# GpSimd in written order, more weights prepared in the output projection, copies behind the mean, and other first loads in a two-layer float32 trunk

## The chip, the cores and the metric

The kernel runs on one core of a Trainium2 chip. The metric is the device time of one execution in microseconds (us). The core's engines are named as in the profile: PE (TensorE; PEld is its weight load), DVE (VectorE), ACT (ScalarE), POOL (GpSimd) and SP (SyncE, which here only issues the loads of weights). A difference of about 0.3% is what a measurement of this kernel can tell from no change.

## What is computed

272 tokens (16 learned ones ahead of 256) of width 1024 go through two layers. Each layer is a gated feed-forward, a mixer, and a second feed-forward, each with a norm before and after it and a residual; the mixer of the first layer is a short convolution, that of the second a differential attention of eight heads. The output is the last 256 tokens.

```python
for i in range(DEPTH):                      # DEPTH = 2
    f = swiglu(rms_norm(h, ln_ffn1[i, 0]), ffn1_w_gu[i], ffn1_w_down[i])
    h = h + 0.5 * rms_norm(f, ln_ffn1[i, 1])
    hn = rms_norm(h, ln_mix[i, 0])
    m = short_conv_mixer(hn, ...) if i == 0 else diff_attention_mixer(hn, ...)
    h = h + rms_norm(m, ln_mix[i, 1])
    f = swiglu(rms_norm(h, ln_ffn2[i, 0]), ffn2_w_gu[i], ffn2_w_down[i])
    h = h + 0.5 * rms_norm(f, ln_ffn2[i, 1])
return h[:, N_META:]
# in diff_attention_mixer, per head: a = softmax(s0) - lam * softmax(s1); o = rms_norm(a @ v) * (1 - lambda_init)
```

## The kernel before

Activations stand transposed: the feature on the 128 partitions, the tokens in the columns. Every product is done in three matmuls per weight tile of 128 by 128: both factors are split into an upper part (`hi`, rounded) and a lower part (`lo`, the rest), and hi*hi, hi*lo and lo*hi are summed in PSUM (`mm3`, L232).

The weights of the twelve products are twelve streams of tiles in the order of their use: `guf0`, `dnf0` (first feed-forward), `cin`, `cout` (convolution), `guf1`, `dnf1`, `guf2`, `dnf2`, `qkv`, `o` (attention), `guf3`, `dnf3`. A chunk of 16 tiles (1 MB) is one load by SP into one of three `raw` buffers; half a chunk, a group of 8 tiles, is prepared by `prepare` (L145): ACT casts `raw` to `hi` (L168), DVE subtracts to get `lo` (L172). There are seven `hi` and seven `lo` buffers. `stream` (L210) runs through the tiles of a stream and calls `prepare` at given places; in the streams `qkv` and `o` that is at the second tile of a group, and at the sixth only if fewer than four groups are ready.

A product that follows a norm begins before the norm's factor is known: for each k (128 features) the first six output tiles are multiplied, six hi*hi, six with the weights' lo, six with the activations' lo (L257, L259, L261). At tile `LATE` (50) the mean comes (`ms`), then its square root on ACT and the reciprocal on DVE, and the outputs are scaled by it (`done`).

At the very start SP loads the eight activation tiles `h` and between them the first 48 weight tiles, six tiles for each k. `guf0`'s first six groups are cast in two halves of four tiles each. 18 small matmuls (`warm_start`) run on PE meanwhile.

The steps of the attention's heads (`Head`) are hung between the tiles of `qkv` and `o` by a table (`HEAD_AT`, `STEPS`): `scores` (`pss`), `most` and `exps` (the softmax), `mix` (the two softmaxes to `w`, on DVE, with a memset of a gap in `w` on POOL), `turn` (PE transposes `w` to `pw`), `turned` (ACT copies it to `wT`), `values` (`po`), `squares` (ACT), `mean` (POOL), `root` (two steps on ACT), `newton` (four small steps on POOL), `scale` (ACT, `o`), `give` (PE transposes `o` to `pt`), `upper`, `lower` (split into the activations of stream `o`). After head 7's `root`, ACT loads the table of the square root, since the next functions need it. At tile 214 DVE takes the reciprocal `rho` of the norm before, and at tiles 216 to 218 and 230 to 234 POOL makes the eight residual tiles `h_f` (`Post.h`, L413) that are needed after the attention.

What sets the order: PE's instructions stand in written order throughout; DVE's and ACT's too in the stretches between `hold` and `let_go`, the attention among them; a scheduler orders POOL's instructions everywhere, and the loads go in the order of `prepare`, as `raw` buffers come free.

Behind the product `o`, `Post` takes the squares of the eight output tiles (ACT), sums them (DVE here, `acc`), sums over partitions by two matmuls with ones (`ms_out`), takes the root (`sz`), and copies the tiles, scaled by a gain, to `f` (L378). The residual, `z`, is formed on DVE from these, and its first tile (`z_f_hi`) starts `guf3`.

Of the kernel before, what the change touches and what calls it, by code (L numbers as in the profile page):

```python
# [14 lines left out]
AF = mybir.ActivationFunctionType  # L15
# [3 lines left out]
P = 128  # L19
# [18 lines left out]
MORE_AT = (2, 6, 7)  # L38
FIRST_AT = (0, 1, 3, 4, 5, 7)
TAIL = 4  # L40
LATER = ("cin", "guf1", "guf2", "qkv", "guf3")
WARM_N = 256
START_WARM = 18
# [49 lines left out]
def trunk_kernel(ctx, tc, a, out):  # L93
# [11 lines left out]
    ctx.enter_context(tc.manual_schedule(engines={mybir.EngineType.PE}))  # L105
    held = []

    def hold():
        if not held:
            held.append(tc.manual_schedule(engines={mybir.EngineType.DVE, mybir.EngineType.Activation}))  # L110
            held[0].__enter__()

    def let_go():
        if held:
            held.pop().__exit__(None, None, None)

    ctx.callback(let_go)
# [33 lines left out]
    def prepare(defer=None):  # L151
        if not queue:
            return
        label, c, g = queue.pop(0)
        if (label, c) not in raws:
            load(label, c)
        raw = raws[label, c]
        hi = wsp.tile([P, HC * P], F32R, tag="hi", name=f"hi_{label}_{c}_{g}")
        lo = wsp.tile([P, HC * P], F32R, tag="lo", name=f"lo_{label}_{c}_{g}")
        both = raw[:, g * HC * P : (g + 1) * HC * P]  # L160

        gain = GAINS[label][:, 0:1] if label in LATER and c == g == 0 else None
        parts = ((0, KO), (KO, HC)) if gain is not None else ((0, HC // 2), (HC // 2, HC)) if label == "guf0" and c < 3 else ((0, HC),)
        for s, e in parts:
            sl = slice(s * P, e * P)
            if gain is None or s:
                with queued(last["sqrt"]):
                    nc.scalar.copy(hi[:, sl], both[:, sl])  # L168

                def lower(sl=sl):  # L170
                    with queued(last["rs"]):
                        nc.vector.tensor_tensor(lo[:, sl], both[:, sl], hi.bitcast(F32)[:, sl], ALU.subtract)  # L172

                lower() if defer is None else defer(lower)
            else:
                nc.scalar.activation(hi[:, sl], both[:, sl], AF.Copy, scale=gain)
                nc.vector.scalar_tensor_tensor(lo[:, sl], both[:, sl], gain, hi.bitcast(F32)[:, sl], ALU.mult, ALU.subtract)
        groups[label, c, g] = hi, lo
# [21 lines left out]
    def at_2(f):  # L200
        at(2, f)

    def run_later(i=None):
        for j in sorted(later) if i is None else (i,):
            for f in later.pop(j, ()):
                f()

    def stream(label, pre=None):
        order = a["streams"][label][1]
        for i, km in enumerate(order):  # L210
# [7 lines left out]
            if label in (*LATER, "guf0") and i <= LATE:  # L218
                pass
            elif label == "qkv" or label == "o":  # L220

                if j == 1 and ahead(label, i) < HIS - 1 or j == 5 and ahead(label, i) < AHEAD and i > LATE + 3 * KD:
                    prepare(at_2)
            elif j == HC // 2 and ahead(label, i) < HIS - 1:
                prepare()
            elif j == 2 and (i > len(order) - 2 * HC and after.get(label) in LATER or ahead(label, i) < AHEAD):
                prepare()
# [62 lines left out]
    for k in range(KD):  # L290
        nc.sync.dma_start(h[k], a["xT"][:, k, :])
        if k == 0:
            nc.scalar.dma_start(gains, a["gains"])
        i, end = k * KO, (k + 1) * KO
        while i < end:
            c, j = divmod(i, CH)
            e = min(CH, j + end - i)
            load("guf0", c, slice(j * P, e * P))
            i += e - j
    small = const.tile([P, 4 * HD + 1], F32, name="small")  # L300
    rope = const.tile([P, 2, T], F32, name="rope")

# [113 lines left out]
    class Pre:  # L416
# [8 lines left out]
        def before(self, i):  # L425
            k, j = divmod(i, KO)
            if i < KD * KO and j == 0:
                if k == 0:
                    run_later()
                    hold()  # L430
                if self.post is None:
                    if k == 0:
# [146 lines left out]
    def attention(name, before, hs):  # L579
# [75 lines left out]
        class Head:  # L655
# [98 lines left out]
            def root(self):  # L754
                _, vv, y, _ = self.st
                nc.scalar.activation(y, vv, AF.Ln)
                nc.scalar.activation(y, y, AF.Exp, scale=-0.5)
                if self.hd == NH - 1:
                    table(AF.Sqrt, y)

            def newton(self):
                _, vv, y, t2 = self.st
# [14 lines left out]
            def upper(self):  # L777
# [2 lines left out]
                lo = actp.tile([P, SEQ], F32R, tag=f"al{hd}", name=f"a_{name}_{hd}_lo")  # L780
                nc.scalar.activation(hi, self.pt[:, :SEQ], AF.Copy, scale=gsub)
                acts[hd] = hi, lo

            def lower(self):
                hi, lo = acts[self.hd]
# [21 lines left out]

        def parts(i):
            if i == LATE:
                for hd, head in enumerate(heads):  # L810
                    for step, late in (STEPS if hd < NH - 1 else LAST_STEPS).items():
                        if hd == NH - 2 and late >= STEPS["values"]:
                            late += 4
                        at(max(HEAD_AT[hd] + late, HEAD_AT[0] - 1) - i, getattr(head, step))
                at(HEAD_AT[0] - 4 - i, by_keys)
# [15 lines left out]
        for i, ((k, m), whi, wlo) in enumerate(stream("o")):  # L831
            xhi, xlo = acts[k]
            mm3(place(m), whi, wlo, xhi, xlo, k == 0 and (m % 2 == 0 or m == KD - 1), k == KD - 1 and (m % 2 == 1 or m == KD - 2))
            if k == KD - 1 and (m % 2 == 1 or m == KD - 2):
                for e in [m] if m >= KD - 2 else [m - 1, m]:
                    post.square(e, place(e))
                    if e == KD - 3:
                        for e in range(2):
                            post.copy(e, place(e))
        post.copies = [lambda m=m: post.copy(m, place(m)) for m in range(2, KD)]  # L840
        return post, pre.hs

    ident = const.tile([P, P], F32, name="ident")
# [118 lines left out]
```

## Time and profile before

| | |
|---|---|
| median of three runs | 1056.34 us (1056.09 to 1059.3) |
| the profiled execution | 1057.03 us; its span, first to last instruction, 1055.3 us |
| PE busy | 1030.3 us, 98% |
| DVE, ACT, POOL busy | 674.4, 545.6, 239.2 us |
| loads | 174.08 MB read, 166 GB/s over the span |
| mean granted TensorE clock | 0.994 |

The profile is one execution. Its times are counted from the span's start; the 1.7 us between span and time lie outside of any instruction. Idle time on PE is what can be won, since the other engines are idle a third of the time or more; a stretch of PE with a lower granted clock counts as busy.

### The profile page before, as it was taken

The page shows a single profiled execution, that of the slowest core. Times are in us where ns is not written, and L with a number is a line of the kernel's source. Part 1 is how long each engine was busy: PE and PEld are TensorE (multiplying, and loading weights), DVE is VectorE, ACT ScalarE, POOL GpSimd, SP SyncE. Part 2 cuts the span into 40 slices and gives each one's busy share as a digit, 9 for nine tenths or more (in the row PEclk, how much of TensorE's full clock was granted, in tenths as well). Part 3 has the DMA queues.
Part 4 walks back from the last instruction along what each step waited for, and adds up shares of the span by engine and source line. Part 5 has one row for each costly group of instructions (what it writes and reads, how often), then busy time and mean ns, then how long its engine had stood idle before and what let it go on. Part 6 is the DMA issues. An engine that isn't in the chain of part 4 may idle for free.

```text
span 1055.3 us, 19380 instructions
## 1 busy us (share of the span) xinstructions
PE 1030.3 (98%) x7948; PEld 1003.9 (95%) x7948; DVE 674.4 (64%) x1062; ACT 545.6 (52%) x968; POOL 239.2 (23%) x262
## 2 busy tenths in 40 slices
PE   8999999999999999999999999999999899999997
PEld 7999999999999999999999999999899788999885
DVE  6776554479858865643687665347977578866442
ACT  6654444454556454444465444444688666544432
POOL 0222211106121522211025221110443403422100
PEclk8999999999999999999999999999999999999999
DMA  8565445425652564454345545442333325654531
GB/s 294 190 218 185 172 165 191 165 81 193 222 186 80 203 217 179 161 185 175 120 150 213 198 160 181 179 162 102 136 126 119 117 81 187 252 200 170 189 141 40
DMA packets 27017, 176.37 MB, mean 167 GB/s; under 512 B 3120, under 2 KB 4528, under 8 KB 6320
## 3 DMA queue, kind: packets, MB, share of 16 engines
q1 hardware_dynamic: 26784, 175.08, 46.3%
q8 instruction: 62, 1.02, 0.4%
q14 instruction: 27, 0.22, 0.1%
q10 hardware_dynamic: 144, 0.06, 0.0%
HBM read 174.08 MB, written 1.05 MB: 166 GB/s over the span
## 4 chain that ended last, share of the span: by engine, by line
PE 90%; DVE 5%; ACT 2%; POOL 1%; issue 1%; DMA 1%; SPq 0%; DVEq 0%
PE ps_guf L234 14%; PE ps_guf L233 14%; PE ps_guf L235 14%; PE ps_dnf L233 6%; PE ps_dnf L234 6%; PE ps_dnf L235 6%; PE ps_out L867 2%; PE ps_out L869 2%; PE ps_out L868 2%; PE ps_guf L259 2%; PE ps_guf L261 2%; PE ps_guf L257 2%; PE ps_cin L233 2%; PE ps_cin L235 2%; PE ps_cin L234 2%; PE ps_qkv L233 1%
## 5 line engine op out<-in xcount | busy, mean ns | idle before, releaser
L235 PE MATMUL ps_guf<-x_f_hi,lo_guf 128*128 128x272 f32 (+1 forms) x1216 | 348.5, 287 | 2.6 <-DVE lo_guf L172 2.6
L233 PE MATMUL ps_guf<-x_f_hi,hi_guf 128*128 128x272 f32 (+1 forms) x1216 | 350.4, 288 | 0.0
L234 PE MATMUL ps_guf<-x_f_lo,hi_guf 128*128 128x272 f32 (+1 forms) x1216 | 349.6, 287 | 0.0
L172 DVE TENSOR_TENSOR lo_guf<-raw_guf,hi_guf 128x1024 fp32r<-128x1024 f32 (+2 forms) x182 | 218.9, 1211 | 61.8 <-ACT hi_guf L168 61.3
L168 ACT CAST hi_guf<-raw_guf 128x1024 fp32r<-128x1024 f32 (+2 forms) x182 | 180.8, 1007 | 133.2 <-PE ps_guf L234 58.0
L235 PEld LDWEIGHTS ps_guf<-x_f_hi,lo_guf 128*128 128x128 f32 x1216 | 229.9, 189 | 3.0 <-DVE lo_guf L172 3.0
L234 PEld LDWEIGHTS ps_guf<-x_f_lo,hi_guf 128*128 128x128 f32 x1216 | 230.9, 190 | 0.1
L233 PEld LDWEIGHTS ps_guf<-x_f_hi,hi_guf 128*128 128x128 f32 x1216 | 229.0, 188 | 0.1
L526 POOL TENSOR_TENSOR sg_f<-sg_f,rs_f 128x272 f32<-128x272 f32 (+1 forms) x88 | 110.4, 1258 | 391.3 <-ACT sg_f L525 391.3
L172 DVE TENSOR_TENSOR lo_dnf<-raw_dnf,hi_dnf 128x1024 fp32r<-128x1024 f32 x88 | 107.9, 1226 | 118.2 <-ACT hi_dnf L168 118.2
L168 ACT CAST hi_dnf<-raw_dnf 128x1024 fp32r<-128x1024 f32 x88 | 92.4, 1050 | 137.6 <-PE ps_dnf L234 65.0
L233 PE MATMUL ps_dnf<-a_f_hi,hi_dnf 128*128 128x272 f32 x528 | 152.1, 288 | 0.0
L234 PE MATMUL ps_dnf<-a_f_lo,hi_dnf 128*128 128x272 f32 x528 | 151.8, 288 | 0.0
L235 PE MATMUL ps_dnf<-a_f_hi,lo_dnf 128*128 128x272 f32 x528 | 151.6, 287 | 0.0
L234 PEld LDWEIGHTS ps_dnf<-a_f_lo,hi_dnf 128*128 128x128 f32 x528 | 99.5, 188 | 0.0
L233 PEld LDWEIGHTS ps_dnf<-a_f_hi,hi_dnf 128*128 128x128 f32 x528 | 99.4, 188 | 0.0
L235 PEld LDWEIGHTS ps_dnf<-a_f_hi,lo_dnf 128*128 128x128 f32 x528 | 99.4, 188 | 0.0
L531 DVE TENSOR_TENSOR av_f<-ps_guf,sg_f 128x272 f32<-128x272 f32 (+1 forms) x88 | 38.3, 435 | 63.5 <-PE ps_guf L235 32.3
L346 POOL TENSOR_TENSOR acc_out_f<-acc_out_f,sq_out_f 128x272 f32<-128x272 f32 x21 | 22.5, 1070 | 157.7 <-ACT sq_out_f L342 157.7
L280 ACT CAST a_f_hi<-av_f 128x272 fp32r<-128x272 f32 (+1 forms) x88 | 36.4, 413 | 36.1 <-DVE av_f L531 36.0
L523 DVE TENSOR_TENSOR g_f<-ps_guf,rs_f 128x272 f32<-128x272 f32 (+1 forms) x88 | 37.3, 432 | 19.3 <-PE ps_guf L235 19.3
L525 ACT ACTIVATE sg_f<-g_f 128x272 f32<-128x272 f32 (+1 forms) x88 | 36.5, 424 | 16.8 <-DVE g_f L523 16.8
(290 smaller groups left out, 1769.7 us busy)
## 6 DMA issues: line engine op xcount, KB each, us to landing
raw_guf<-in_guf SPq DMA_DIRECT2D x85, 1024.0 KB, 4.8
raw_dnf<-in_dnf SPq DMA_DIRECT2D x44, 1024.0 KB, 4.8
raw_cin<-in_cin SPq DMA_DIRECT2D x12, 1024.0 KB, 4.8
raw_qkv<-in_qkv SPq DMA_DIRECT2D x12, 1024.0 KB, 4.8
raw_cout<-in_cout SPq DMA_DIRECT2D x4, 1024.0 KB, 4.8
raw_o<-in_o SPq DMA_DIRECT2D x4, 1024.0 KB, 4.9
raw_guf<-in_guf SPq DMA_DIRECT2D x6, 384.0 KB, 5.4
h<-in_xT SPq DMA_DIRECT2D x8, 136.0 KB, 5.4
```

What stands on the lines that cost most here:

```text
L168: nc.scalar.copy(hi[:, sl], both[:, sl])
L172: nc.vector.tensor_tensor(lo[:, sl], both[:, sl], hi.bitcast(F32)[:, sl], ALU.subtract)
L233: nc.tensor.matmul(o, whi, xhi, start=start, stop=False)
L234: nc.tensor.matmul(o, whi, xlo, start=False, stop=False)
L235: nc.tensor.matmul(o, wlo, xhi, start=False, stop=stop)
L257: nc.tensor.matmul(o, hi, xhi, start=start, stop=False)
L280: nc.scalar.copy(hi, x)
L346: self.eng.tensor_tensor(self.acc[:, :n], self.acc[:, :n], sq[:, :n], ALU.add)
L523: nc.vector.tensor_tensor(g[:, :n], p, pre.r, ALU.mult)
L525: nc.scalar.activation(s[:, :n], g[:, :n], AF.Silu)
L526: nc.gpsimd.tensor_tensor(s[:, :n], s[:, :n], pre.r, ALU.mult)
L531: nc.vector.tensor_tensor(v[:, :n], p, keep.pop(j)[:, :n], ALU.mult)
```

## The change

Five things are changed.

1. **First loads.** The six tiles of the first k are loaded in two pieces, tiles 0 and 1 and then tiles 2 to 5 (`FIRST_LOADS`); later pieces are the same. The casts of `guf0`'s first groups are cut where the loads are cut, instead of into halves.
2. **POOL in written order** from tile `LATE` of `qkv` to the start of `guf3` (`hold` with the engine Pool, `let_go(1)`).
3. **Head 0 later.** Head 0's steps from `turn` on come four tiles later.
4. **More weights in `o`.** `prepare` is called at the sixth tile of each group of `o` too, as long as fewer than six groups are ready; for the last eight tiles the DVE half is put off by sixteen tiles, behind the sums of the squares.
5. **Around the mean behind `o`.** All copies `f` come behind the mean (before, two stood among the squares); the load of the square root's table stands behind head 7's `upper` instead of its `root`.

```diff
+FIRST_LOADS = (2, 6, 12, 18, 24, 30, 36, 42, 48)
-        parts = ((0, KO), (KO, HC)) if gain is not None else ((0, HC // 2), (HC // 2, HC)) if label == "guf0" and c < 3 else ((0, HC),)
+        i0 = c * CH + g * HC
+        if label == "guf0":
+            cuts = sorted({0, HC} | {i - i0 for i in FIRST_LOADS if 0 < i - i0 < HC})
+        else:
+            cuts = (0, HC) if gain is None else (0, KO, HC)
...
-                if j == 1 and ahead(label, i) < HIS - 1 or j == 5 and ahead(label, i) < AHEAD and i > LATE + 3 * KD:
-                    prepare(at_2)
+                if ahead(label, i) < HIS - 1 and (j == 1 or j == 5 and (label == "o" or ahead(label, i) < AHEAD and i > LATE + 3 * KD)):
+                    prepare(at_2 if label != "o" or i < len(order) - HC else at_joint)
...
                 if k == 0:
                     run_later()
+                    let_go(1)
                     hold()
...
                 nc.scalar.activation(y, y, AF.Exp, scale=-0.5)
-                if self.hd == NH - 1:
-                    table(AF.Sqrt, y)
...
                 nc.scalar.activation(hi, self.pt[:, :SEQ], AF.Copy, scale=gsub)
                 acts[hd] = hi, lo
+                if hd == NH - 1:
+                    table(AF.Sqrt, self.st[2])
...
             if i == LATE:
+                hold((mybir.EngineType.Pool,))
...
-                        if hd == NH - 2 and late >= STEPS["values"]:
+                        if hd == NH - 2 and late >= STEPS["values"] or hd == 0 and late >= STEPS["turn"]:
                             late += 4
...
-                    if e == KD - 3:
-                        for e in range(2):
-                            post.copy(e, place(e))
-        post.copies = [lambda m=m: post.copy(m, place(m)) for m in range(2, KD)]
+        post.copies = [lambda m=m: post.copy(m, place(m)) for m in range(KD)]
```

ACT at the start of the program. `hi_guf0_0_0` is the first group of eight tiles, `x_f0_1_hi` the activations of the second k. Before:

```order
L283 ACTIVATE x_f0_0_hi_151<-h0_78,gains_86 128x272
L168 CAST hi_guf0_0_0_155<-raw_guf0_0_89 128x512 x2
L283 ACTIVATE x_f0_1_hi_161<-h1_79,gains_86 128x272
L168 CAST hi_guf0_0_1_165<-raw_guf0_0_89 128x512 x2
L283 ACTIVATE x_f0_2_hi_171<-h2_80,gains_86 128x272
```

After:

```order
L292 ACTIVATE x_f0_0_hi_152<-h0_78,gains_86 128x272
L174 CAST hi_guf0_0_0_156<-raw_guf0_0_89 128x256
L174 CAST hi_guf0_0_0_156<-raw_guf0_0_89 128x512
L174 CAST hi_guf0_0_0_156<-raw_guf0_0_89 128x256
L292 ACTIVATE x_f0_1_hi_164<-h1_79,gains_86 128x272
```

The group is cast in pieces of two, four and two tiles; the first two pieces are the six tiles of the first k, and the last piece is the one that needs the second load.

POOL in the last head. `st_6` and `st_7` are the statistics of heads 6 and 7 (first row the mean, the others `newton`), `h_f2_0` to `h_f2_7` the residual tiles. Before:

```order
L766 TENSOR_TENSOR st_6_10067<-st_6_10067 128x2
L413 TENSOR_TENSOR h_f2_0_10128<-f_f2_0_7914,rho_f2_10114 128x272
L413 TENSOR_TENSOR h_f2_1_10133<-f_f2_1_7996,rho_f2_10114 128x272
L413 TENSOR_TENSOR h_f2_2_10141<-f_f2_2_8084,rho_f2_10114 128x272
L413 TENSOR_TENSOR h_f2_3_10216<-f_f2_3_8170,rho_f2_10114 128x272
L413 TENSOR_TENSOR h_f2_4_10221<-f_f2_4_8258,rho_f2_10114 128x272
L413 TENSOR_TENSOR h_f2_5_10229<-f_f2_5_8340,rho_f2_10114 128x272
L413 TENSOR_TENSOR h_f2_6_10237<-f_f2_6_8429,rho_f2_10114 128x272
L413 TENSOR_TENSOR h_f2_7_10246<-f_f2_7_8522,rho_f2_10114 128x272
L752 TENSOR_TENSOR st_7_10163<-st_7_10163,stat_7_10013 128x2
```

After:

```order
L775 TENSOR_TENSOR st_6_10082<-st_6_10082 128x2
L423 TENSOR_TENSOR h_f2_0_10145<-f_f2_0_7917,rho_f2_10131 128x272
L423 TENSOR_TENSOR h_f2_1_10150<-f_f2_1_7999,rho_f2_10131 128x272
L423 TENSOR_TENSOR h_f2_2_10158<-f_f2_2_8087,rho_f2_10131 128x272
L763 TENSOR_TENSOR st_7_10180<-st_7_10180,stat_7_10022 128x2
L772 TENSOR_TENSOR st_7_10180<-st_7_10180 128x2
L773 TENSOR_TENSOR st_7_10180<-st_7_10180 128x2
L774 TENSOR_SCALAR st_7_10180<-st_7_10180 128x2
L775 TENSOR_TENSOR st_7_10180<-st_7_10180 128x2
L423 TENSOR_TENSOR h_f2_3_10230<-f_f2_3_8173,rho_f2_10131 128x272
```

Head 7's five small steps stand behind three residual tiles instead of eight.

DVE behind the last head, up to the first sums of the squares (`acc_out_at`). `w_7` is head 7's mix, `lo_o_3_0`, `lo_o_3_1` and `lo_guf3_...` are lower halves of weights. Before:

```order
L715 SCALAR_TENSOR_TENSOR w_7_10077<-e_7_1_10017,stat_7_10013,e_7_0_10014 128x272
L716 SCALAR_TENSOR_TENSOR stat_7_10013<-stat_7_10013 128x2
L172 TENSOR_TENSOR lo_o_3_0_10085<-raw_o_3_10082,hi_o_3_0_10084 128x1024
L409 RECIPROCAL rho_f2_10114<-sz_f2_8548 128x272
L172 TENSOR_TENSOR lo_o_3_1_10136<-raw_o_3_10082,hi_o_3_1_10135 128x1024
```

After:

```order
L178 TENSOR_TENSOR lo_o_3_1_10063<-raw_o_3_10036,hi_o_3_1_10062 128x1024
L720 RECIPROCAL stat_7_10022<-stat_7_10022 128x2
L721 SCALAR_TENSOR_TENSOR stat_7_10022<-stat_7_10022,nlam_8540 128x2
L726 SCALAR_TENSOR_TENSOR w_7_10092<-e_7_1_10026,stat_7_10022,e_7_0_10023 128x144
L726 SCALAR_TENSOR_TENSOR w_7_10092<-e_7_1_10026,stat_7_10022,e_7_0_10023 128x272
L727 SCALAR_TENSOR_TENSOR stat_7_10022<-stat_7_10022 128x2
L183 SCALAR_TENSOR_TENSOR lo_guf3_0_0_10100<-raw_guf3_0_10097,gains_86,hi_guf3_0_0_10099 128x768
L178 TENSOR_TENSOR lo_guf3_0_0_10100<-raw_guf3_0_10097,hi_guf3_0_0_10099 128x256
L419 RECIPROCAL rho_f2_10131<-sz_f2_8551 128x272
```

The last weights of `o` come ahead of head 7's mix, and the first group of `guf3` ahead of the reciprocal `rho`. From here on the preparing stands two groups further: where `lo_guf3_1_1` stood among the sums, `lo_guf3_2_1` now stands behind them, and every group of `guf3` that follows stands two groups earlier than before.

## Rows read from the trace of the kernel before

**Rows 1.** PE's waits over the span: who waited for whom, sum, times, longest (us)

```profile
PE pt L775 <- ACT o L770: 4.1, 1, 4.1
PE ps_guf L257 <- ACT hi_guf L168: 3.8, 3, 2.4
PE ps_guf L235 <- DVE lo_guf L172: 2.6, 2, 1.6
...
PE pw L724 <- DVE w L715: 1.4, 1, 1.4
PE ms_out_at L355 <- DVE acc_out_at L346: 1.3, 1, 1.3
```

**Rows 2.** Timeline of PE at the start: start, duration (us), [idle before <- releaser]

```profile
1.19 3.77 PE L126 MATMUL warm_start<-warmer 128*128 128x256 bf16 x18 [1.19 <-DVE warmer L311]
6.15 0.76 PE L257 MATMUL ps_guf<-x_f_hi,hi_guf 128*128 128x272 f32 x4 [1.19 <-ACT hi_guf L168]
9.29 0.82 PE L257 MATMUL ps_guf<-x_f_hi,hi_guf 128*128 128x272 f32 x2 [2.38 <-ACT hi_guf L168]
...
12.63 1.56 PE L257 MATMUL ps_guf<-x_f_hi,hi_guf 128*128 128x272 f32 x6
...
29.38 0.28 PE L233 MATMUL ps_guf<-x_f_hi,hi_guf 128*128 128x272 f32 x1
```

**Rows 3.** Timeline of ACT at the start

```profile
5.48 0.62 ACT L168 CAST hi_guf<-raw_guf 128x512 fp32r<-128x512 f32 x1 [1.62 <-DMA raw_guf<-in_guf]
8.62 0.62 ACT L168 CAST hi_guf<-raw_guf 128x512 fp32r<-128x512 f32 x1 [2.53 <-DMA raw_guf<-in_guf]
9.15 0.52 ACT L283 ACTIVATE x_f_hi<-h,gains 128x272 fp32r<-128x272 f32 x1
```

**Rows 4.** Stretches: length, busy us (instructions) by engine, granted TensorE clock, DMA

```profile
8.00:14.80 6.80, 5.51 (x24) 5.51 (x25) 5.48 (x11) 5.91 (x13) 0.00 (x0) 0.50 0.97 305
```

**Rows 5.** The same view in another answer: a late start stretch, and behind the longest wait

```profile
14.20:30.00 15.80, 15.80 (x125) 15.80 (x125) 10.16 (x19) 8.13 (x18) 0.23 (x1) 0.98 0.90 341
...
841.00:844.20 3.20, 3.16 (x15) 3.08 (x16) 2.25 (x4) 2.60 (x4) 0.00 (x0) 0.50 0.00 0
```

**Rows 6.** Loads issued in the first 32 us: count, KB, median us to landing

```profile
raw_guf<-in_guf SPq DMA_DIRECT2D x6, 384.0 KB, 5.4
...
raw_guf<-in_guf SPq DMA_DIRECT2D x2, 128.0 KB, 5.6
```

**Rows 7.** Chain that ended last, merged (start, us, what), in the attention

```profile
765.34 0.63 ACT o L749 x4
```

**Rows 8.** Timeline of DVE in head 1 and around the last head

```profile
766.93 1.23 DVE L172 TENSOR_TENSOR lo_qkv<-raw_qkv,hi_qkv 128x1024 fp32r<-128x1024 f32 x1 [1.72 <-ACT hi_qkv L168]
...
828.71 1.85 DVE L409 RECIPROCAL rho_f<-sz_f 128x272 f32<-128x272 f32 x1
```

**Rows 9.** Timeline of POOL around the last head

```profile
827.95 0.90 POOL L763 TENSOR_TENSOR st<-st 128x2 f32<-128x2 f32 x1 [1.08 <-ACT st L757]
...
830.63 6.83 POOL L413 TENSOR_TENSOR h_f<-f_f,rho_f 128x272 f32<-128x272 f32 x8 [0.96 <-DVE rho_f L409]
837.43 0.19 POOL L752 TENSOR_TENSOR st<-st,stat 128x2 f32<-128x2 f32 x1
```

**Rows 10.** Timeline of ACT behind the last head

```profile
838.11 1.28 ACT L317 ACT_TABLE_LOAD   x1
```

**Rows 11.** Timeline of PE: head 7's last transposes, and two waits in guf3

```profile
841.04 0.73 PE L775 MATMUL pt<-ident,o 128*128 128x128 f32 x2 [4.12 <-ACT o L770]
...
869.30 0.50 PE L257 MATMUL ps_guf<-x_f_hi,hi_guf 128*128 128x256 f32 x2 [0.27 <-ACT hi_guf L168]
...
878.37 0.39 PE L235 MATMUL ps_guf<-x_f_hi,lo_guf 128*128 128x256 f32 x1 [0.99 <-DVE lo_guf L172]
```

**Rows 12.** Timeline of DVE at the mean behind o

```profile
850.27 1.22 DVE L172 TENSOR_TENSOR lo_guf<-raw_guf,hi_guf 128x1024 fp32r<-128x1024 f32 x1
851.41 1.48 DVE L346 TENSOR_TENSOR acc_out_at<-acc_out_at,sq_out_at 128x256 f32<-128x256 f32 x3
```

More of the change, by code (lines that the diff above doesn't have):

```diff
@@ L106, in trunk_kernel, with hold, let_go @@
     held = []
[L108 to L114, printed above, removed]
+    def hold(engines=(mybir.EngineType.DVE, mybir.EngineType.Activation)):
+        if not held or mybir.EngineType.Pool in engines:
+            held.append(tc.manual_schedule(engines=set(engines)))
+            held[-1].__enter__()
+    def let_go(n=0):
+        while len(held) > n:
             held.pop().__exit__(None, None, None)
@@ L162, in prepare @@
         gain = GAINS[label][:, 0:1] if label in LATER and c == g == 0 else None
-        parts = ((0, KO), (KO, HC)) if gain is not None else ((0, HC // 2), (HC // 2, HC)) if label == "guf0" and c < 3 else ((0, HC),)
-        for s, e in parts:
+        i0 = c * CH + g * HC
[3 more added lines that the diff above has]
+            cuts = (0, HC) if gain is None else (0, KO, HC)
+        for s, e in zip(cuts, cuts[1:]):
             sl = slice(s * P, e * P)
@@ L201, in at_2, with at_joint @@
         at(2, f)
+    def at_joint(f):
+        at(2 * HC, f)
     def run_later(i=None):
@@ L293, in trunk_kernel @@
             nc.scalar.dma_start(gains, a["gains"])
[L294 to L299, printed above, removed]
+        i = k * KO
+        for end in FIRST_LOADS:
+            while i < end <= (k + 1) * KO:
+                c, j = divmod(i, CH)
+                e = min(CH, j + end - i)
+                load("guf0", c, slice(j * P, e * P))
+                i += e - j
     small = const.tile([P, 4 * HD + 1], F32, name="small")
```

## The prediction

> **What bounds the kernel now.** I read the busy times first: PE is busy 98% of the span, the next engine, DVE, 674.4 of 1055.3 us, 64% (table above). So no other engine's speed is worth anything in itself; what can be won is PE's idle time and the time that it works at the lower clock. The waits of PE come next [rows 1]. The reader is to see that a few places make up most of it: 4.1 us in front of head 7's last transposes, 3.8 at the start (three waits for cast weights, the largest 2.4), 2.6 for the lower halves of `guf3`'s weights, 1.4 for head 0's mix and 1.3 for the sum behind `o`. Then the timeline of each engine at those places, to see what is late there and what stands behind it, and last the stretches with their granted clock: it is 0.50, the lower of the two levels (1.2 GHz), from 8.0 to 14.8 us, behind two idle stretches of 1.19 and 2.38 us [rows 2, 4], and again from 841.0 to 844.2, behind the idle 4.12 us [rows 5, 11]. At the upper level 125 matmuls take 15.8 us, 0.126 each; at the lower, 24 take 5.51 us and 15 take 3.16, so 0.230 and 0.211 each [rows 4, 5].
>
> **First loads.** Before, the first k's tiles 4 and 5 are cast together with 6 and 7, which come with the second load. So PE does four matmuls at 6.15 and stands until 9.29, although all six tiles lay in SBUF when the cast of 5.48 began; k = 1 begins at 12.63 and tile 48 at 29.38 [rows 2, 3]. Now tiles 0 and 1 are a load of their own, which hides behind the warm-up (until 1.19 + 3.77 = 4.96), and tiles 2 to 5 are cast together. Their load holds the last bytes of what was one load, so I let it land when that did; the sixteen matmuls that are left run from 6.15 on without a wait and are over between 6.15 + 16 x 0.126 = 8.2 and 6.15 + 16 x 0.230 = 9.8. Now k = 1 waits for the second load, 8.62, then for a cast of two tiles (half of 0.62) and for its activations, 0.52: 9.5, and I take 9.6 [rows 3]. What follows to tile 48 is 7 x 18 = 126 matmuls. At the upper level throughout they end at 9.6 + 126 x 0.126 = 25.5, 3.9 earlier than before. If the lower level lasts to 14.8 as now, 5.2 us do 23 of them and the other 103 take 13.0: 27.8, 1.6 earlier. The idle stretches get shorter (about 1.2 and 1.3 instead of 1.19 and 2.38), but they are still there, so I take 2.5. The piece more costs SP one issue; should it put the second load off by half a microsecond, 1.1 is left. Ends: 1.1 and 3.9.
>
> The trace shows 5.6 us from issue to landing for 128 KB and 5.4 for 384 KB there [rows 6]: in a full queue size hardly matters. The Trainium skill (DMA: Bandwidth & Descriptors, Rules for kernel authors, and Latency and other measured facts) speaks against the cut: small transfers should be joined into large ones, and some 2 us of every load are fixed. Paid in series before the second load, they would move k = 1 to 11.6, and the start would bring 0.5 by estimate; the rows show no such step between loads, but none shows a cut load either.
>
> **Head 0, four tiles later.** PE's wait of 1.4 us for `w` goes, since four tiles are 12 x 0.126 = 1.5 us of work [rows 1, 5]. But head 1's mix stands next on DVE, and DVE there waits 1.72 us for a cast on ACT [rows 8]: it doesn't follow PE. Only the 0.63 us of head 0's squares, which now stand behind that cast, make it earlier [rows 7]. So 0.6 of the 1.4 is kept. I count none of it by itself: before head 7's transposes it is lost again, as follows.
>
> **Last head.** Two things move its chain. Later: `rho` now stands behind one group of weights more on DVE, 1.2 us like any such step [rows 12], and head 7's mix behind another. `rho` ended at 828.71 + 1.85 = 830.56; I let it end at 832.0 [rows 8]. Earlier: POOL then makes three residual tiles instead of eight, each 6.83 / 8 = 0.85 [rows 9], and reaches head 7's mean at 832.0 + 2.6 = 834.6 instead of 837.43. From that mean to the transposes it took 841.04 - 837.43 = 3.6, with the table load of 1.28 in it, which now stands behind [rows 9 to 11]; 2.3 is left, and with the steps between engines I take 2.5. So the transposes start at 837.1. PE is there at 841.04 - 4.12 = 836.9. The wait falls from 4.1 to 0.2: 3.9 gained. Ends: 4.7 if `rho` is no later (the whole wait and the 0.6 of head 0), and 1.9 if POOL is held up as in the first rival. The table load is covered by the time in which PE finishes `o`, some 24 tiles; the root needs it only behind them.
>
> **Clock behind it.** Where PE waits 0.2 instead of 4.12 us, it should not fall to the lower level; the wait of 1.4 [rows 1] lies in no stretch of lower clock. The 15 matmuls from 841.0 to 844.2 then cost 15 x (0.211 - 0.126) = 1.3 less [rows 5]. The end below: nothing, if some 3 us of wait remain.
>
> **Mean behind `o`.** DVE's group of weights at 850.27 (1.22) stands in front of the last three sums [rows 12]; now it stands behind them. Together with the two copies that leave ACT's squares this makes the sum earlier by about 1.2, and PE's wait there is 1.3 [rows 1]: 1.2 gained, ends 0.6 and 1.3. The seven copies that now follow the root are covered by DVE's chain, which takes them one by one; the group moved behind the sums just fits into the time of mean and root.
>
> **Weights for `guf3`.** They are prepared two groups earlier, 16 tiles or some 5.6 us of PE. The waits of 0.27 and 0.99 [rows 11], a second of 1.6 for lower halves (2.6 in all [rows 1]) and a short one of 0.3 beside the first go: 3.2. What is late next are the sums and gates of the first outputs, which no wait in the trace shows. Ends: 2.4 and 3.2. The casts that come earlier in `o` lie on ACT and DVE; where they delay a head is counted above.
>
> **Sum.** 2.5 + 3.9 + 1.3 + 1.2 + 3.2 = 12.1. From the profiled execution, 1057.03, that is 1044.9; it lies 0.7 above the median of the three runs, 1056.34, so I predict 1056.3 - 12.1 = 1044.2.
>
> **Rivals.** First, the stall at head 7 shrinks less. A small POOL step took 0.90 us beside DVE's weights and 0.19 elsewhere [rows 9], and head 7's five steps now stand beside two groups on DVE. Two or three blocked steps of 0.7 make 2.0: 1046.2. For it speaks the one row; against it that DVE waits for ACT's casts between its groups. The Trainium skill (SBUF — State Buffer, Who interferes with whom) states it as a rule: a DVE instruction with two SBUF inputs and a GpSimd instruction that reads SBUF exclude each other for the whole instruction. By it each of two groups blocks once at most its own 1.2 us, about 2.4 by estimate; the row agrees that there is blocking, not that every step meets it.
>
> Second, the start gives little: the second load lands later or the lower clock lasts as long as before. 1.1 instead of 2.5: 1045.6; with nothing at all 1046.7. For it speaks that both idle stretches remain.
>
> Third, the earlier weights find no room: a `hi` buffer is free only when PE is done with the group seven before, a `raw` buffer only when its lower halves are made. Then `guf3`'s 3.2 us remain: 1047.4. Against it: in `o` the casts stand behind steps that PE has passed by then.
>
> Fourth, and slower than before: POOL in written order. The memset in each `w` was far ahead of its need; now it stands behind POOL's work of the head before, and POOL's small steps wait for ACT (1.08 us of idle time before one of them [rows 9]). Where POOL reaches it after PE has reached that head's transposes, PE waits. It decides from 2.2 us per head: seven heads are then 15.4, 12.1 of gain are gone and the time is 1059.6. Against it: POOL is busy 239.2 of 1055.3 us, 23% (table above).
>
> Fifth, the changes don't do what they say: the order shows them in place, so I give this nothing.
>
> **How the numbers follow.** Forecast 0.62, first rival 0.14, second 0.12, third 0.05, several of them together so that under 0.3% (3.2 us) is left 0.03, fourth 0.04. Faster by over 0.3%: 0.62 + 0.14 + 0.12 + 0.05 = 0.93; within 0.3% (about what a measurement of this kernel can tell from no change) 0.03; slower 0.04. The low end takes the best of each term, 3.9 + 4.7 + 1.3 + 1.3 + 3.2 = 14.4: 1041.9. The high end takes the worst of all but the clock, 1.1 + 1.9 + 1.3 + 0.6 + 2.4 = 7.3: 1049.0, which covers the first three rivals one at a time.
>
> **What would show it.** In the profile after: no wait of PE of 2 us at the start, tile 48 at 26.9; a wait at head 1's `w` of about 0.8 where head 0's was; head 7's transposes with a wait under 1 us and a clock of 1.0 behind them; no wait at the sum behind `o`; none for `guf3`'s weights. I am wrong if PE waits at the heads' transposes for POOL, or if a long wait stands again at `pt`.

## The result and the profile after

The changed kernel takes 1043.5 us (median of four runs, 1043.07 to 1043.75), the kernel before 1056.5 beside it: a ratio of 0.9871, with a 95% interval of 0.9853 to 0.9888, or 13.0 us less. The forecast was 1044.2, 12.1 less. The profiled execution took 1043.29 us, its span is 1041.5.

PE's waits over the span, after; they answer to [rows 1]. Behind the colon stand sum, times, longest.

```profile
PE ps_guf L266 <- DVE z_f_hi L412: 1.8, 3, 0.7
PE warm_start L128 <- DVE warmer L321: 1.2, 1, 1.2
PE ps_guf L266 <- ACT hi_guf L174: 1.0, 1, 1.0
PE pw L735 <- DVE w L726: 0.9, 1, 0.9
PE ms_out_at L365 <- DVE acc_out_at L356: 0.7, 1, 0.7
...
PE ps_guf L266 <- ACT x_f_hi L292: 0.4, 1, 0.4
```

Gone are the 4.1 us for `pt` and all of `guf3`'s waits for weights. Of 3.8 at the start 1.4 are left, of 1.3 at the sum behind `o` 0.65, and head 0's wait has become one at head 1.

The start, on PE and then on ACT (to be held against [rows 2, 3]), and the same stretch as [rows 4] with one behind head 7's transposes (length, then busy us by engine, granted clock, DMA):

```profile
4.94 0.52 PE L266 MATMUL ps_guf<-x_f_hi,hi_guf 128*128 128x272 f32 x2
6.49 0.77 PE L266 MATMUL ps_guf<-x_f_hi,hi_guf 128*128 128x272 f32 x4 [1.03 <-ACT hi_guf L174]
...
9.10 1.28 PE L266 MATMUL ps_guf<-x_f_hi,hi_guf 128*128 128x272 f32 x6 [0.35 <-ACT x_f_hi L292]
...
25.22 0.28 PE L242 MATMUL ps_guf<-x_f_hi,hi_guf 128*128 128x272 f32 x1
```

```profile
5.82 0.62 ACT L174 CAST hi_guf<-raw_guf 128x512 fp32r<-128x512 f32 x1 [0.93 <-DMA raw_guf<-in_guf]
8.21 0.41 ACT L174 CAST hi_guf<-raw_guf 128x256 fp32r<-128x256 f32 x1 [1.78 <-DMA raw_guf<-in_guf]
```

```profile
8.00:14.80 6.80, 6.45 (x49) 6.02 (x49) 5.92 (x12) 6.40 (x15) 0.00 (x0) 1.00 0.95 338
832.50:835.70 3.20, 3.14 (x26) 3.02 (x27) 1.18 (x2) 2.75 (x6) 3.20 (x4) 1.00 0.20 84
```

In the 6.8 us in which PE did 24 matmuls before it does 49. Tile 48 begins at 25.22 instead of 29.38. Behind the transposes 26 matmuls stand in 3.2 us, where there were 15.

The last head: POOL, the reciprocal on DVE, and PE's transposes (against [rows 8, 9, 11]).

```profile
824.12 0.92 POOL L773 TENSOR_TENSOR st<-st 128x2 f32<-128x2 f32 x1
...
827.17 3.20 POOL L423 TENSOR_TENSOR h_f<-f_f,rho_f 128x272 f32<-128x272 f32 x3 [1.51 <-DVE rho_f L419]
830.34 0.19 POOL L763 TENSOR_TENSOR st<-st,stat 128x2 f32<-128x2 f32 x1
```

```profile
823.98 1.01 DVE L183 SCALAR_TENSOR_TENSOR lo_guf<-raw_guf,gains,hi_guf 128x768 fp32r<-128x768 f32 x1
...
825.25 1.84 DVE L419 RECIPROCAL rho_f<-sz_f 128x272 f32<-128x272 f32 x1
```

```profile
832.56 0.59 PE L784 MATMUL pt<-ident,o 128*128 128x128 f32 x2
...
842.54 0.70 PE L365 MATMUL ms_out_at<-acc_out_at,ones 128*128 128x256 f32 x2 [0.65 <-DVE acc_out_at L356]
...
845.22 1.50 PE L266 MATMUL ps_guf<-z_f_hi,hi_guf 128*128 128x256 f32 x6 [0.68 <-DVE z_f_hi L412]
```

Matched instruction by instruction on PE, the two traces tell where the time went. A matmul's start before less the same one's after is what has been gained up to there:

| PE is at | before | after | gained so far | this part |
|---|---|---|---|---|
| tile 48 of `guf0` | 29.38 | 25.22 | 4.2 | 4.2, and constant up to the attention |
| `pw` of head 1 | 768.96 | 764.33 | 4.6 | 0.5, head 0 |
| scores of head 7 | 819.41 | 814.92 | 4.5 | -0.1 |
| `pt` of head 7 | 841.04 | 832.56 | 8.5 | 4.0, the last head |
| 15 matmuls further | 844.31 | 834.52 | 9.8 | 1.3, the clock |
| sum behind `o` | 852.94 | 842.54 | 10.4 | 0.6, the mean |
| `guf3`'s sixth matmul | 856.22 | 846.33 | 9.9 | -0.5 |
| behind the last wait for weights | 886.17 | 872.01 | 14.2 | 4.3, the weights |

### The profile page after: what moved, and what is told of

It is laid out like the page before. It is cut to its first block, busy times and chain, and to the rows that moved or that the text cites. A ratio compares the mean times of both kernels' runs of the same rounds, so it can differ in the third digit from the quotient of the medians.

```text
span 1041.5 us, 19396 instructions
## 1 busy us (share of the span) xinstructions
PE 1026.4 (99%) x7948; PEld 1000.0 (96%) x7948; DVE 674.5 (65%) x1063; ACT 546.8 (52%) x969; POOL 240.7 (23%) x262
## 4 chain that ended last, share of the span: by engine, by line
PE 92%; DVE 4%; ACT 2%; issue 1%; DMA 1%; POOL 1%; SPq 0%; DVEq 0%
PE ps_guf L243 15%; PE ps_guf L242 15%; PE ps_guf L244 14%; PE ps_dnf L242 6%; PE ps_dnf L243 6%; PE ps_dnf L244 6%; PE ps_guf L266 2%; PE ps_guf L270 2%; PE ps_guf L268 2%; PE ps_out L876 2%; PE ps_out L878 2%; PE ps_out L877 2%; PE ps_cin L242 2%; PE ps_cin L244 2%; PE ps_cin L243 2%; PE ps_qkv L242 1%
## 5 line engine op out<-in xcount | busy, mean ns | idle before, releaser
L178 DVE TENSOR_TENSOR lo_guf<-raw_guf,hi_guf 128x1024 fp32r<-128x1024 f32 (+3 forms) x183 | 219.2, 1205 | 65.2 <-ACT hi_guf L174 64.7
L174 ACT CAST hi_guf<-raw_guf 128x1024 fp32r<-128x1024 f32 (+3 forms) x183 | 181.2, 1002 | 130.4 <-PE ps_guf L243 56.4
```

## The experiments

All kernels but one are the changed kernel with an edit. Medians are of four runs. Those of the kernel before beside them lie between 1056.7 and 1057.7, so two medians are told apart from about one microsecond on; what is smaller is read from the traces, by matched matmuls as above.

**The start undone.** `FIRST_LOADS` without its 2, and

```diff
-            cuts = sorted({0, HC} | {i - i0 for i in FIRST_LOADS if 0 < i - i0 < HC})
+            cuts = (0, HC // 2, HC) if c < 3 else (0, HC)
```

> The changed kernel with the first loads and the casts of guf0 as before (one load of six tiles, casts in halves of four); everything else stays. Theory A, the start's gain is carried through to the end: tile 48 moves back from 25.2 to 29.4 us, PE's waits of 1.2 and 2.4 us and the granted clock of 0.50 up to about 14.8 us come back, and the time rises by 4.1 us, from 1043.5 to 1047.6. Theory B, what the start gains is lost in part at the next place where PE waits (as the prediction thought of head 0's gain): 2.5 us or less come back, at most 1046.0.

Measured 1046.64, 3.1 more; tile 48 at 28.02, 2.8 later, and the 2.8 are still there at the last matmul. So the start's gain is carried to the end (A), but it is smaller than the 4.2 of the pair above. The same loads and casts as before gave 28.02 here and 29.38 in the trace of before; here the second load was there at 7.76 instead of 8.62, and the upper level came at 12.9 us instead of 14.8. PE's timeline in this run:

```profile
8.43 0.82 PE L266 MATMUL ps_guf<-x_f_hi,hi_guf 128*128 128x272 f32 x2 [1.14 <-ACT hi_guf L174]
9.04 1.56 PE L268 MATMUL ps_guf<-x_f_hi,lo_guf 128*128 128x272 f32 x6
10.40 1.56 PE L270 MATMUL ps_guf<-x_f_lo,hi_guf 128*128 128x272 f32 x6
11.76 1.40 PE L266 MATMUL ps_guf<-x_f_hi,hi_guf 128*128 128x272 f32 x6
13.00 0.92 PE L268 MATMUL ps_guf<-x_f_hi,lo_guf 128*128 128x272 f32 x6
```

Six matmuls take 1.36 us from start to start (0.227 each) up to about 12.9 and 0.76 behind it: the lower level, then the upper.

**One load, the casts cut.** `FIRST_LOADS` without its 2, the cuts as changed: one load of six tiles, a cast of six, a cast of two.

> The changed kernel with one load for the first six tiles, as before, but with the casts cut at tile 6 (six tiles in one cast, then two). Theory A, it is the cast that no longer waits for the second load that gives the start's gain: the six tiles are cast in about 0.85 us from 5.5 us on, PE stands 1.4 us once, k = 1 starts at 9.1 and the time stays within 0.4 us of 1043.5. Theory B, the small first load gives it, because its two matmuls shorten PE's idle time: with one idle stretch of 1.4 us instead of 1.03 the clock falls to 0.50 for some us, and 1.7 to 2.5 us come back, 1045.2 to 1046.0. Theory C, the load more costs an issue: with one fewer the second load lands earlier and the time falls to 1043.0.

1044.04, 0.5 more (A allowed 0.4), and tile 48 at 25.83: nearly the whole gain without the small load, so A in kind. The lower level lasted to 9.5 us (the first six matmuls take 1.73 us), which looks like B; but it lasted to 10.0, 10.1 and 10.6 in three of the runs below that have the small load (on the cast, on head 0 and on the table load), and their tile 48 came at 25.9, 26.3 and 26.3. So B isn't shown, and the 0.6 us of this trace lie within that scatter. The second load came at 8.69, not earlier than the 8.21 beside the small load: against C.

**PE kept busy in the gaps.** The start as in the first run, with `START_WARM` 22 and, between the fourth and the fifth matmul,

```diff
+                        if label == "guf0" and i < KO and nth == 4:
+                            warm(GAP_WARM, "gap", first_bank)
```

> The changed kernel with the first loads and casts as before, as in the run on the start, but with four more warm-up matmuls ahead and eight between PE's fourth and fifth matmul of the program, so that PE does not stand in its two gaps. Theory A, the time at the lower clock is a consequence of PE's idle stretches: the clock is up by 6.5 us and stays, tile 48 comes at 26.2 to 26.8 instead of 28.0, and the time is about 1.5 us below the run without the extra matmuls, 1045.0. Theory B, the clock's rise does not follow these stretches: tile 48 stays at 27.6 to 28.4 or comes later by the 0.3 us that the extra matmuls take, 1046.6 to 1047.0.

1044.61, 2.0 under the first run (A), although the second load came late, at 8.37. PE from the fourth matmul on:

```profile
6.61 1.05 PE L129 MATMUL warm_start<-warmer 128*128 128x256 bf16 x8
9.04 0.51 PE L270 MATMUL ps_guf<-x_f_hi,hi_guf 128*128 128x272 f32 x2 [1.39 <-ACT hi_guf L176]
9.39 0.91 PE L272 MATMUL ps_guf<-x_f_hi,lo_guf 128*128 128x272 f32 x6
```

It waits 1.39 us there and goes on at the upper level. With the first loads as before, all three traces (before, the first run, POOL's order alone) ran at the lower level up to 12.9 to 14.8 us (before from 8.0 on) and had tile 48 at 28.0 to 29.4; with the changed ones seven traces (the changed kernel and the six runs that keep its start) had it at 24.6 to 26.3, at the upper level from 10.7 us at the latest. The means, 28.8 and 25.4, make the start 3.4 us. The length of the wait alone doesn't tell the level: among the seven the longest first waits, 1.45 us each, went with the upper level from 4.1 us on in one run (the mean as before) and only from 10.1 in another (head 0), and the shortest, 0.75, with 10.0. What decides within this start is not shown.

**POOL not in written order.**

```diff
-                hold((mybir.EngineType.Pool,))
```

> The changed kernel without POOL's written order; the scheduler puts six residual tiles ahead of head 7's mean and two more ahead of its newton steps, and all memsets of w early. Theory A, POOL's place for the residual tiles makes the wait in front of head 7's transposes: five tiles of 0.94 to 1.07 us stand ahead of the last steps instead of behind them, PE waits 3.5 to 5 us at pt, the clock falls to 0.50 behind it for some 3 us (1.2 us more), and the time is 1048.2 to 1049.5. Theory B, the table load and the earlier weights had made the wait: it stays under 1 us and the time is within 1 us of 1043.5.

1048.24. The wait is back, and the lower clock behind it (PE, then the stretch):

```profile
835.75 0.73 PE L784 MATMUL pt<-ident,o 128*128 128x128 f32 x2 [3.97 <-ACT o L779]
```

```profile
836.00:839.00 3.00, 3.00 (x15) 3.00 (x15) 0.48 (x1) 2.46 (x4) 0.00 (x0) 0.50 0.00 0
```

**POOL's order alone**, put into the kernel before (the same `hold`, and `let_go(1)`).

> The kernel before with POOL's written order alone. Theory A: it is worth the whole of the last head's term: rho at 830.6 as before, three residual tiles, head 7's mean at 833.3 to 833.9 instead of 837.4, and with the table load and a cast still on ACT ahead of the scale PE's wait at pt falls from 4.1 to 0.2 to 0.7 us; the stretch of clock 0.50 behind it goes too, 1.3 us; gain 4.7 to 5.2, 1051.3 to 1051.9. Theory B: without the table load behind the root's place, POOL's order alone leaves a wait of 2 us or more at pt and gains under 3 us. Theory C, the slower rival of the prediction: memsets of w come late and PE waits at several heads' transposes: over 1056.

1051.63, a ratio of 0.9947 (0.9931 to 0.9962). `pt` waits 0.5 us, head 7's mean stands at 833.82 instead of 837.43, and PE gains 3.6 us there and 1.3 by the clock. That is A; the slower rival (C) is out, no head waits for POOL's memset.

**The table load back behind the root.**

```diff
+                if self.hd == NH - 1:
+                    table(AF.Sqrt, y)
...
-                if hd == NH - 1:
-                    table(AF.Sqrt, self.st[2])
```

> The changed kernel with the load of the square root's table back behind head 7's root (ahead of the scale) instead of behind its upper. Theory A: POOL's newton steps take 1.0 us from 831.1 on and ACT fills them with a cast of 1.03; the table (1.28 + 0.20) would push cast and scale back, so PE waits 1.3 to 1.6 us at head 7's transposes, the clock stays at the upper level, and the time is 1044.8 to 1045.2. Theory B: the wait goes into the slack of the mean behind o, which is bound by ACT's squares: under 0.5 us, 1043.9.

1044.06. The wait at `pt` is 1.30 us, as A says, without a lower clock; the sum behind `o` then waits 0.40 instead of 0.65, so 1.0 us is lost in the trace. The median shows about half of that, within its scatter.

**The weights in `o` as before.**

```diff
-                if ahead(label, i) < HIS - 1 and (j == 1 or j == 5 and (label == "o" or ahead(label, i) < AHEAD and i > LATE + 3 * KD)):
-                    prepare(at_2 if label != "o" or i < len(order) - HC else at_joint)
+                if j == 1 and ahead(label, i) < HIS - 1 or j == 5 and ahead(label, i) < AHEAD and i > LATE + 3 * KD:
+                    prepare(at_2)
```

> The changed kernel with the old condition for preparing weights in o (second tile of a group, sixth only below four groups); POOL's order, the copies and the start stay. Theory A, guf3's waits came from weights two groups too late: 3.2 us of waits for hi_guf and lo_guf come back, the sum behind o waits 1.3 instead of 0.65 us because a group stands among the sums again, and the time is 1043.5 + 3.2 + 0.6 = 1047.3. Theory B, the waits came from head 7's lateness, which shifted the casts behind it: with that gone they stay small, and the time is 1044.1 or less.

1047.97 (A). Three of the four waits for weights stand again, at the same matmuls as before; the one of 0.27 for a cast doesn't. The sum behind `o` waits 1.27 again.

```profile
861.01 0.51 PE L268 MATMUL ps_guf<-x_f_hi,lo_guf 128*128 128x256 f32 x2 [0.29 <-DVE lo_guf L178]
...
868.84 0.39 PE L244 MATMUL ps_guf<-x_f_hi,lo_guf 128*128 128x256 f32 x1 [0.99 <-DVE lo_guf L178]
...
876.41 0.39 PE L244 MATMUL ps_guf<-x_f_hi,lo_guf 128*128 128x256 f32 x1 [1.61 <-DVE lo_guf L178]
```

From the first `z` to the last matmul it takes 3.9 us longer than the changed kernel; the later sum adds 0.6.

**Head 0 at its old tiles.**

```diff
-                        if hd == NH - 2 and late >= STEPS["values"] or hd == 0 and late >= STEPS["turn"]:
+                        if hd == NH - 2 and late >= STEPS["values"]:
```

> The changed kernel with head 0's steps back at their old tiles. Theory A, as the prediction counted it: what head 0 gains is lost again before head 7's transposes, so nothing is lost here: PE waits 1.4 us for head 0's w and nothing for head 1's, comes to head 7's transposes 0.4 us later and waits there no longer than now; time within 0.2 of 1043.5. Theory B: head 7's chain is no longer the bound (PE waits 0.09 us there now), so head 0's net gain of about 0.45 us counted in the changed kernel: the difference of PE's place before and behind heads 0 and 1 stays to the end, 1044.0.

1043.61; the median can't tell. In the trace PE waits 1.41 at head 0's `w`, not at head 1's, and 0.6 us are lost there and stay lost to the end: B.

**The mean as before.** Copies 0 and 1 again behind the sixth square, and `at_joint` replaced by `at_2`.

> The changed kernel with the mean behind o as before: two copies f among ACT's squares, and the last group's lower half on DVE ahead of the last three sums (it is lo_guf3_2_1 now). The weights stay as changed. Theory A, the prediction's term of 1.2 us: the sum is later by the group on DVE (1.22) or the copies on ACT (0.9), PE's wait for it rises from 0.65 to 1.6 to 1.9 us, and 1.0 to 1.2 us are lost there, 1044.6. Theory B, what stands now among the squares (a cast of 1.05) sets the sum anyway and both edits are worth half a microsecond together at most: a wait of 0.7 to 1.2, 1044.0.

1043.3: no loss that the median shows. PE in this run, and below it the row of the kernel before that answers to its second one:

```profile
842.85 0.70 PE L365 MATMUL ms_out_at<-acc_out_at,ones 128*128 128x256 f32 x2 [1.59 <-DVE acc_out_at L356]
...
845.44 0.97 PE L266 MATMUL ps_guf<-z_f_hi,hi_guf 128*128 128x256 f32 x6 [0.59 <-DVE z_f_hi L412]
```

```profile
855.53 0.97 PE L257 MATMUL ps_guf<-z_f_hi,hi_guf 128*128 128x256 f32 x6 [0.59 <-DVE z_f_hi L402]
```

The wait for the sum grows by 0.94, as A says. But the first six matmuls of `guf3` take 0.97 us here and 1.50 in the changed kernel, which gives half of it back: 0.5 is left in the trace. Both theories had looked at the sum alone.

**The cast out of the squares.** No `prepare` in the last eight tiles of `o`, one more behind the first `z`.

```diff
+                if label == "o" and i >= len(order) - HC:
+                    pass
...
-                    for _ in range(MORE_AT.count(k)):
+                    for _ in range(MORE_AT.count(k) + (k == 0 and self.post.name == "at")):
```

> The changed kernel without the group of weights that is prepared in the last eight tiles of o (its cast of 1.05 us stands among ACT's squares); it comes behind the first z of guf3 instead. Theory A, this cast is what is left of the wait behind o: squares and sums follow PE, PE's wait for the sum falls from 0.65 to under 0.15 us, guf3 has no wait for weights, and the time falls by 0.5 us, to 1043.0. Theory B, DVE's seven sums in a row (3.6 us, behind two groups of weights) set it: the wait stays over 0.4.

1043.5, and the wait for the sum is still 0.66. A is wrong, B's number holds. ACT, and then DVE:

```profile
838.89 1.59 ACT L354 ACTIVATE sq_out_at<-ps_o 128x256 f32<-128x256 f32 x4 [1.07 <-PE ps_o L246]
841.02 1.12 ACT L354 ACTIVATE sq_out_at<-ps_o 128x256 f32<-128x256 f32 x3 [0.53 <-PE ps_o L246]
842.44 0.38 ACT L354 ACTIVATE sq_out_at<-ps_o 128x256 f32<-128x256 f32 x1 [0.31 <-PE ps_o L246]
```

```profile
836.90 2.82 DVE L178 TENSOR_TENSOR lo_guf<-raw_guf,hi_guf 128x1024 fp32r<-128x1024 f32 x2 [1.97 <-ACT hi_guf L174]
839.65 3.59 DVE L358 TENSOR_TENSOR acc_out_at<-acc_out_at,sq_out_at 128x256 f32<-128x256 f32 x7
```

ACT is not late: its last squares wait for PE itself. The sum that PE waits for holds seven of the eight squares (the eighth goes to PE by itself), and the seventh is done at 842.14, but DVE's seventh sum ends at 843.24. The seven sums follow one another without a stop, 0.53 us apart, and the first begins when the two groups of weights are done, although its square has been there since 839.28. So DVE's row of sums behind these groups sets the wait here, as B says. Two other runs agree: with the table load back and with POOL free, DVE's groups end earlier against PE, the first sum begins 0.35 us earlier against PE's last product of `o`, and the wait is 0.40 and 0.41, with the cast in place. How far it would fall if no group stood there was not run.

**Four edits at once**: that cast, head 1 four tiles later too (`hd < 2`), the second k's activations ahead of the cast of two tiles, five warm-up matmuls in the gap of 1.03.

> The changed kernel with four edits at the places where PE still waits: the cast out of the squares, as in the run beside this one (0.5 us); head 1 four tiles later too (its wait of 0.94 us); the activations of the second k ahead of the cast of the last two tiles of the first group (PE's wait of 0.35 us there); five warm-up matmuls in the gap of 1.03 us between PE's second and third matmul of the program. Theory A, each counts by itself: tile 48 at 24.4 to 24.8 with the clock up before 7 us, no wait for a head's w, 0.6 kept there, 0.5 at the mean: 1041.6. Theory B, the gains of head 1 and of the mean are lost at the next place where PE waits, and the start is within the scatter that the runs show (24.6 to 26.3): 1042.8 or more.

1044.3, slower than the changed kernel if anything. Head 1's wait of 0.94 is gone, and these two stand in its place:

```profile
766.57 0.59 PE L794 MATMUL pt<-ident,o 128*128 128x128 f32 x2 [0.82 <-ACT o L789]
...
778.04 0.59 PE L794 MATMUL pt<-ident,o 128*128 128x128 f32 x2 [1.00 <-ACT o L789]
```

Between tile 48 (24.95) and the last matmul 1.45 us are lost against the changed kernel. B, and more than B.

**Copies back ahead of the mean, without the cast**, and the second k's activations earlier.

```diff
                     post.square(e, place(e))
+                    if e == 3:
+                        for e in range(2):
+                            post.copy(e, place(e))
```

> The changed kernel with three edits: no group of weights among the last squares (as in the run that moved that cast), the first two copies f back ahead of the mean, in the place on ACT that this frees (behind the fourth square), and the activations of the second k ahead of the cast of the last two tiles of the first group. Theory A, the copies behind the mean hold the PSUM banks that guf3's fifth and sixth matmul need: with two copies ahead of the mean the first six matmuls of guf3 take 0.97 us instead of 1.50, the wait for the sum stays at 0.65, so 0.5 us are gained there, and 0.35 at the second k: 1042.6. Theory B, the six matmuls are slow for another reason (the weights' loads, the clock): they stay at 1.50 and only the start's 0.35 is gained: 1043.2.

1042.95 (ratio 0.9863, 0.9847 to 0.9880), the lowest median, though 0.5 us under the changed kernel's is less than medians tell apart. The trace has the step:

```profile
842.35 0.70 PE L370 MATMUL ms_out_at<-acc_out_at,ones 128*128 128x256 f32 x2 [0.66 <-DVE acc_out_at L361]
...
844.94 0.98 PE L271 MATMUL ps_guf<-z_f_hi,hi_guf 128*128 128x256 f32 x6 [0.59 <-DVE z_f_hi L417]
```

The six matmuls are back to 0.98 with the sum as early as in the changed kernel (A); with the cast out and the copies left behind the mean, in the run on the cast, they took 1.50, so it is the copies. From tile 48 to the last matmul 0.3 us are gained, net. At the second k nothing is: PE waits 0.33 there for the cast instead of 0.35 for the activations.

## Why the prediction was right, point by point

**First loads: 2.5 forecast, 4.2 in the pair of traces, 3.4 as a mean.** The step that was too small is the clock's: I let the lower level last in part because idle stretches of 1.2 and 1.3 us remained. The first did (1.03), the second shrank to 0.35, since the second load was there at 8.21 instead of 8.62 and PE began the sixteen matmuls later, at 6.49; and 49 matmuls instead of 24 stand in the stretch up to 14.8. The price that the prediction put on the rule against small loads (the Trainium skill, DMA: Bandwidth & Descriptors, Rules for kernel authors), 2 us more before the second load, does not show: its cast began at 7.5 to 8.3 in the seven traces with one load more and at 7.8 to 8.9 in the five without it. That tile 48 moves by more than a microsecond from one execution to the next (24.6 to 26.3 with the same start) I had not seen: one trace gives a start to about 1 us only.

**Head 0: counted 0, worth 0.5.** The 0.94 at head 1 (0.8 forecast) and the 0.5 kept are right; "lost again before head 7" is wrong. That holds while PE waits at head 7's transposes. With that wait gone, PE comes first there and what is gained before counts, as the run with head 0 at its old tiles shows.

**Last head: 3.9 forecast, 4.0.** Shifted by the 4.5 that PE is ahead there, `rho` ends at 831.6 (forecast 832.0), head 7's mean stands at 834.8 (834.6), the transposes at 837.05 (837.1). POOL's order alone brings 3.6 of it, and the table load alone is worth 1.2 at that place; together that is more than 4.0, since `rho` ends 1.0 later than before (831.6 and 830.56). The first rival's mechanism is there too: a small step of POOL took 0.92 us from 824.12 on, beside DVE's group of 823.98 to 824.99, and the three residual tiles took 3.20 instead of 2.6. One of them took 1.75, up to 829.64, beside DVE's group from 827.29 to 829.01, which itself took 1.72 instead of 1.22; the other two took 0.76 and 0.77. That agrees with the rule cited (the Trainium skill, SBUF — State Buffer, Who interferes with whom). The 0.85 per tile of the prediction was a mean over eight with one such tile among them (1.75 from 832.08 on, before). The 0.6 that this costs three tiles was nearly made up by `rho`, which ended 0.4 earlier than forecast.

**Clock behind it: 1.3 forecast, 1.3.** Shown from both sides: it goes with the wait in POOL's order alone and returns with it when POOL is free.

**Mean behind `o`: 1.2 forecast, 0.1.** Two steps failed. The step "this makes the sum earlier by about 1.2" took the group that stood among the sums for the whole delay; against PE's last product of `o` the last sum ends only 0.6 earlier. DVE before, and then after:

```profile
848.34 2.02 DVE L346 TENSOR_TENSOR acc_out_at<-acc_out_at,sq_out_at 128x256 f32<-128x256 f32 x4 [2.73 <-ACT sq_out_at L342]
```

```profile
836.15 2.83 DVE L178 TENSOR_TENSOR lo_guf<-raw_guf,hi_guf 128x1024 fp32r<-128x1024 f32 x2 [1.97 <-ACT hi_guf L174]
838.90 3.59 DVE L356 TENSOR_TENSOR acc_out_at<-acc_out_at,sq_out_at 128x256 f32<-128x256 f32 x7
```

Before, the first sum waited for its square, and the group split the seven into four and three [rows 12]. Now the seven stand in one row of 3.59 us, but two groups of weights, there because the preparing is earlier, stand in front of it, and the first sum begins 0.35 us later against PE. That leaves a wait of 0.65. And "the seven copies are covered by DVE's chain" is wrong: they hold PSUM banks. Copies 5 and 6, the last readers of the third and the fourth bank, end at 845.92 and 846.28, and the fifth and the sixth matmul of `guf3` start at 845.97 and 846.33; in the kernel before these follow the fourth without a stop. That takes 0.5 of the 0.6 back. (With the earlier weights in place the sum would wait 1.59 without the two edits, so against that they bring 0.5.)

**Weights for `guf3`: 3.2 forecast, 4.3.** The mechanism is as told, and no new wait appeared. The size was off because I added up idle times: see below. Undoing the weights alone gives back 3.9 behind the first `z`, not 4.3; the fourth wait, for a cast, doesn't come back, so whether it came from the weights is not shown.

**Rivals.** The second (a start that gives little) and the third (no room for earlier weights) did not come; the fourth is out by POOL's order alone. The sum, 12.1, is near the 13.0 measured since the mean's 1.1 too much stands against 0.9 too little at the start (by its mean), 0.5 at head 0 and 1.1 at the weights; with these the traces make it 13.5. Two of the five terms, the mean and the weights, lie outside the ends that the prediction gave them, in opposite directions, so that the sum came so near is in part luck.

## What to carry to other kernels

A long wait in front of one instruction is often another engine's order: ask what stands ahead of the late step on the engine that releases it, and move only that. Where a sum is made step by step on another engine, ask when the first step can begin and how long the row of steps is, before counting a step taken out of it as gain; and ask of every copy that is put off which buffer it sets free. A tile later in one place pays only until the next step of the same chain is late, so look at that step first.

## What was not expected of the hardware

A wait costs PE more than the idle time that the profile lists: that counts from the end of the matmul before, whose record is 0.28 us long although matmuls start 0.12 apart. In the kernel before, the wait of 0.99 us [rows 11] stands between matmuls that start at 877.10 and 878.37, 1.27 apart instead of 0.12, and the next one comes 0.22 later: 1.25 in all. The four waits for `guf3`'s weights, 3.16 us by the list, cost 4.3.

A wait for a PSUM bank may not be listed at all: the 0.5 us lost by `guf3`'s fifth and sixth matmul appear as no wait, only as a row of six matmuls that takes 1.50 instead of 0.97.

The granted clock in the stretches can't be trusted at the program's start. In the run with the start undone the two stretches below both say 1.00, though PE does 11 matmuls in the first and 18 in the second; the pace tells the level.

```profile
10.00:12.00 2.00, 2.00 (x11) 2.00 (x11) 1.95 (x5) 1.73 (x5) 0.00 (x0) 1.00 1.05 343
14.00:16.00 2.00, 2.00 (x18) 2.00 (x17) 2.00 (x5) 2.00 (x6) 0.00 (x0) 1.00 1.06 406
```
